# Queueing ScalarE's evacuating copies behind the newest high part, with a look-ahead of six chunks in some stages and four in the others, in an fp32 encoder trunk

## The chip, the cores and the metric

The kernel runs on one core of a Trainium2 chip. The metric is the device time of one execution in microseconds (us). TensorE (PE) multiplies, VectorE (DVE) and ScalarE (ACT) work on what goes into and comes out of the products, GpSimd (POOL) does a few additions, and SyncE (SP) issues most of the DMAs.

## What is computed

The reference is a trunk of two residual layers over 256 tokens of width 2048. Layer 0 mixes tokens by neighbourhood attention, layer 1 by a gated short convolution; each is followed by a gated MLP of inner width 5632. Everything is float32.

```python
def conv_glu_ffn(x, w_up, conv_w, conv_b, w_down):
    h = dwconv_centered(x @ w_up, conv_w) + conv_b
    g, u = jnp.split(h, 2, axis=-1)
    return (jax.nn.silu(g) * u) @ w_down
...
def reference(x, ...):
    h = x
    for i in range(DEPTH):
        a = rms_norm(h, mix_norm[i])
        ...                               # neighborhood_attention, or short_conv_mixer
        h = h + mixed
        h = h + conv_glu_ffn(rms_norm(h, ffn_norm[i]), ffn_w_up[i], ffn_conv_w[i], ffn_conv_b[i], ffn_w_down[i])
    return rms_norm(h, final_norm)
```

## The kernel before

**Numbers in two parts.** Each float32 operand is split into a high part, which ScalarE makes by a cast to a shorter format (the weights' at L185, the activations' at L301), and a low part, the rest, which VectorE makes by a subtraction (L188, L302). A product is the sum of three: high by high, high by low, low by high.

**Chunks.** All weights pass through the core as one list of chunks of 512 KB, in the order in which they are used. For each chunk `prep_to` (L130) writes down a load by SP into one of six `raw` buffers (L164), the cast by ScalarE into one of six `hi` buffers (L185), and the subtraction by VectorE into one of six `lo` buffers (L188). The loads stand in a fixed order on SP's queue. 64 entries of the list are no chunks but jobs ("make", L193): they load three quarter tiles, form three sums on VectorE (L207 to L209) and store them (L214); later stages read the sums back as "kept" chunks.

**Two kinds of stage.** In a `Phase` (L228) the weights are the stationary operand and the 256 tokens stream past them; this is the form of the query and key products (`wqk`), of the short convolution's input (`wsc`) and of the four halves of the up-projections (`wup`: two layers by two halves). An item of a `Phase` is mostly a pair of output tiles: four chunks, 32 matmuls of 512 columns with the high parts (L262), then 32 of 256 columns with the low parts (L270). Each output tile owns one of four `mm` accumulators. In `Values` (L665) and `Tokens` (L387) the activations are stationary and the weights stream: the value products, the attention output, the convolution's output and the four halves of the down-projections (L460 to L462, L686 to L688). Some `Tokens` items (`seven`) take three chunks, one of them kept, and do seven products in place of eight.

**Evacuation.** When an output tile of a `Phase` is done, `both` (L319) evacuates it: ScalarE copies the second half of the accumulator out (L322, tile `corr`), and VectorE adds the first half to it (L323). In the up-projections a chain follows (`up_evac`): scaling (L328), convolution (L336 on ScalarE, L338 twice on VectorE), the gate (L742, L745), the split of the result (L301, L302), and for every second pair of tiles the sums that a `seven` needs (`make_forms`, L517, on POOL) with their splits.

**What sets the order.** The body of L916 to L934 walks the items: it prepares what the item itself needs, writes down its products and evacuations, and then prepares on until `AHEAD` chunks beyond the item's end (jobs do not count). From all that is written down, a scheduler at compile time makes the order of each engine's instructions; the written order is a priority in it, not the order itself. `issue_after(x)` forces an instruction to stand behind `x` on their common engine; it adds no wait on another engine. `newest["ACT"]` is the cast that was written down last. In stages with `self.fence` (every `Phase` but `wqk`) the list `fenced` is filled while an evacuation is written down (L273 to L276), and the splits at L301 and L302 already stand behind the newest cast and the newest subtraction:

```python
            if fenced:
                for x in ("ACT", "DVE"):
                    order.enter_context(tc.issue_after(newest[x].ins))
```

An evacuation is written down before its item's own preparation ahead. With a look-ahead of six, the newest cast is then the one of the second chunk of the following item.

Of the kernel before, what the change touches and what calls it, by code (L numbers as in the profile page):

```python
# [24 lines left out]
S = 256  # L25
# [7 lines left out]
QSCALE = float(128 ** -0.5)  # L33

CH = 8
AHEAD = 6

INTRO = 4
STEP = 4
# [40 lines left out]
def trunk(ctx, tc, xT, par, bias, wqk, wv, wo, wsc, wscout, wup, wdown, out):  # L80
    nc = tc.nc
# [42 lines left out]
    ends = []  # L124
# [5 lines left out]
    def prep_to(n):  # L130
        while len(prepped) < min(n, len(chunks)):
            src, w, kind = chunks[len(prepped)]
            for due in [x for x in stores if x[0] <= len(prepped)]:
                stores.remove(due)
                due[1]()
            if kind == "make":
                make(*src)
                prepped.append(())
                continue
            raw = wp.tile([P, CH * P], F32, name="raw", tag="raw", bufs=RAWS)  # L140
            if kind == "rows":
                load(raw[:, :w], src)
                prepped.append(parts(raw[:, :w]) + (raw,))
                continue

            if kind == "kept":
                t42, left, sums = prepped[-1][2], prepped[-2][2], src()
                load(t42[:, 4 * P:], sums[:, 8 * P:])
                load(raw, sums[:, :8 * P])
                nc.vector.tensor_add(out=t42[:, :4 * P].rearrange("p (f c) -> p f c", f=4),  # L150
                                     in0=t42[:, 4 * P:].rearrange("p (f c) -> p f c", f=4),
                                     in1=left.rearrange("p (f k c) -> p k f c", f=4, c=P)[:, 1])
                prepped.append((parts(raw), parts(t42)))
                continue

            load(raw[:, :4 * w].rearrange("p (f c) -> p f c", f=4), src.rearrange("f p c -> p f c"))
            prepped.append(parts(raw[:, :4 * w].rearrange("p (f k c) -> p f k c", f=4, c=P)) + (raw,))
# [10 lines left out]
    def parts(r):  # L168

        both, low = high_part(r)  # L170
        low()
        return both
# [18 lines left out]
    kept, newest, fenced = {}, {}, []  # L191
# [92 lines left out]
    item = [0]  # L284
    at = [0]

    def tick():
        due = [x for x in later if x[0] <= at[0]]
        later[:] = [x for x in later if x[0] > at[0]]
        for _, fn in due:  # L290
            fn()
        at[0] += 1
# [26 lines left out]
    def both(ps, tag="corr"):  # L319

        corr = tp.tile([P, S], F32, name="corr", tag=tag)
        nc.scalar.copy(out=corr, in_=ps[:, S:])  # L322
        nc.vector.tensor_add(out=corr, in0=ps[:, :S], in1=corr)  # L323
        return corr

    def normed(dst, ps):

        nc.vector.tensor_mul(out=dst, in0=both(ps), in1=rstd)  # L328
# [252 lines left out]
    def qk_evac(f, ps):  # L581
        c = both(ps, "g" if waiting and len(held) % 2 else "corr")
        if waiting:
            held.append(lambda: qk_rest(f, c))
        else:
            qk_rest(f, c)
# [329 lines left out]
    for item[0], (ph, ft, c, k0, ka, kb) in enumerate(items):  # L916

        with ExitStack() as order:
            for x in factor_at:
                order.enter_context(tc.issue_after(x.ins))  # L920
            prep_to(ends[item[0]])
            done = ph.run(ft, c, k0, ka, kb)
            if item[0] != KT // STEP * INTRO:

                if done:
                    order.enter_context(tc.issue_after(done.ins))
                end, n = ends[item[0]], AHEAD
                while n and end < len(chunks):
                    n -= chunks[end][2] != "make"
                    end += 1  # L930
                prep_to(end)
        if item[0] > KT // STEP * INTRO:
            factor_at.clear()
        tick()  # L934
# [70 lines left out]
```

## Time and profile before

| what | value |
|---|---|
| time, median of 3 runs | 2221.36 us (2219.43 to 2226.04) |
| time of the profiled execution | 2221.64 us |
| its span, first to last instruction | 2219.5 us |
| mean granted TensorE clock | 0.996 |
| loads of `raw`, casts L185, subtractions L188 | 920 each |
| copies L322 | 256, of which 224 in fenced stages |

In the profile's timeline a row is: start, duration, engine, line, operation, tiles (out<-in), shape, count, and in brackets the idle time of that engine before it with what ended it. PE is the matmul row of TensorE; its rows overlap a little, since a matmul's end is modelled. SPq and ACTq are DMA issues. A row with a count merges equal neighbours.

The stages of interest lie at these times in the profiled execution: first up-projection half about 397 to 649 us, second 759 to 1010, `wsc` 1126 to 1395, third up-projection half 1481 to 1733, fourth 1843 to 2093. Between them lie `Tokens` stages; queries, keys, values and attention come before 306 us.

### The profile page before, as it was taken

The page shows a single profiled execution, that of the slowest core. Times are in us where ns is not written, and L with a number is a line of the kernel's source. Part 1 is how long each engine was busy: PE and PEld are TensorE (multiplying, and loading weights), DVE is VectorE, ACT ScalarE, POOL GpSimd, SP SyncE. Part 2 cuts the span into 40 slices and gives each one's busy share as a digit, 9 for nine tenths or more (in the row PEclk, how much of TensorE's full clock was granted, in tenths as well). Part 3 has the DMA queues.
Part 4 walks back from the last instruction along what each step waited for, and adds up shares of the span by engine and source line. Part 5 has one row for each costly group of instructions (what it writes and reads, how often), then busy time and mean ns, then how long its engine had stood idle before and what let it go on. Part 6 is the DMA issues. An engine that isn't in the chain of part 4 may idle for free.

```text
span 2219.5 us, 33399 instructions
## 1 busy us (share of the span) xinstructions
PE 2186.1 (98%) x11716; PEld 1891.2 (85%) x11716; DVE 1852.2 (83%) x2842; ACT 1306.1 (59%) x1985; POOL 128.6 (6%) x155
## 2 busy tenths in 40 slices
PE   9999999999999999999999999999999999999998
PEld 8888888888888888888888888888888888888886
DVE  8787667799888978888888777888888898888787
ACT  7555556566665645566655455565666665566565
POOL 0000000001100001210000010000100000010000
PEclk9999999999999999999999999999999999999999
DMA  8777557589758879967778887766986787897575
GB/s 292 231 253 235 188 175 226 195 303 310 250 197 262 284 235 315 316 225 245 247 254 282 292 285 239 236 231 211 301 278 196 231 282 236 293 314 248 182 263 171
DMA packets 362072, 555.34 MB, mean 250 GB/s; under 512 B 21680, under 2 KB 249136, under 8 KB 361904
## 3 DMA queue, kind: packets, MB, share of 16 engines
q1 hardware_dynamic: 332880, 502.23, 69.3%
q10 hardware_dynamic: 29024, 50.98, 6.0%
q8 instruction: 92, 1.51, 0.3%
q14 instruction: 76, 0.62, 0.1%
HBM read 500.70 MB, written 52.43 MB: 249 GB/s over the span
## 4 chain that ended last, share of the span: by engine, by line
PE 84%; DVE 6%; DMA 3%; ACT 3%; issue 2%; POOL 1%; SPq 0%; ACTq 0%; DVEq 0%
PE mm L262 35%; PE mm L270 18%; PE mm L460 6%; PE mm L461 6%; PE mm L462 6%; PE mu L460 3%; DVE lo L188 3%; PE mu L461 3%; PE mu L462 3%; DMA raw<-in_wup 2%; ACT hi L185 2%; PE mm L688 1%; PE mm L686 1%; PE mm L687 1%; DVE conv L338 1%
## 5 line engine op out<-in xcount | busy, mean ns | idle before, releaser
L188 DVE TENSOR_TENSOR lo<-raw,hi 128x1024 fp32r<-128x1024 f32 (+1 forms) x856 | 1019.3, 1211 | 167.5 <-ACT hi L185 74.4
L185 ACT CAST hi<-raw 128x1024 fp32r<-128x1024 f32 (+1 forms) x920 | 918.6, 1012 | 377.8 <-PE mm L462 137.3
L262 PE MATMUL mm<-a,hi 128*128 128x512 f32 x4096 | 970.9, 392 | 17.3 <-ACT hi L185 14.4
L262 PEld LDWEIGHTS mm<-a,hi 128*128 128x128 f32 x4096 | 761.3, 189 | 172.6 <-ACT hi L185 18.1
L270 PEld LDWEIGHTS mm<-a,lo 128*128 128x128 f32 x4096 | 514.5, 191 | 14.0 <-DVE lo L188 1.4
L270 PE MATMUL mm<-a,lo 128*128 128x256 f32 x4096 | 520.1, 283 | 1.1 <-DVE lo L188 1.1
L460 PE MATMUL mm<-hi,act 128*128 128x512 f32 x634 | 247.7, 391 | 2.0 <-ACT hi L185 1.2
L462 PE MATMUL mm<-hi,act 128*128 128x512 f32 x634 | 246.7, 389 | 0.0
L461 PE MATMUL mm<-lo,act 128*128 128x512 f32 x576 | 224.5, 390 | 0.0
L338 DVE SCALAR_TENSOR_TENSOR conv<-pad,pt,conv 128x256 f32<-128x256 f32 x384 | 182.1, 479 | 26.4 <-ACT conv L336 21.2
L322 ACT COPY corr<-mm 128x256 f32<-128x256 f32 x256 | 92.4, 370 | 189.6 <-PE mm L270 185.7
L336 ACT ACTIVATE conv<-pad,pt 128x256 f32<-128x256 f32 x176 | 105.7, 601 | 147.6 <-DVE pad L328 144.8
L460 PEld LDWEIGHTS mm<-hi,act 128*128 128x128 f32 x634 | 119.0, 188 | 28.3 <-DVE corr L323 1.6
L462 PEld LDWEIGHTS mm<-hi,act 128*128 128x128 f32 x634 | 119.0, 188 | 24.7
L461 PEld LDWEIGHTS mm<-lo,act 128*128 128x128 f32 x576 | 108.2, 188 | 21.7
L323 DVE TENSOR_TENSOR corr<-mm,corr 128x256 f32<-128x256 f32 x256 | 106.6, 417 | 19.6 <-ACT corr L322 18.9
L526 POOL TENSOR_TENSOR s<-conv 128x128 f32<-128x128 f32 x27 | 38.4, 1423 | 1018.9 <-DVE conv L745 1018.9
L302 DVE TENSOR_TENSOR act<-conv,act 128x256 fp32r<-128x256 f32 x88 | 39.3, 446 | 50.1 <-ACT act L301 49.9
L328 DVE TENSOR_TENSOR pad<-corr,rstd 128x256 f32<-128x256 f32 x176 | 73.8, 420 | 1.1
L461 PE MATMUL mu<-lo,sf 128*128 128x512 f32 x180 | 70.0, 389 | 0.0
L462 PE MATMUL mu<-hi,sf 128*128 128x512 f32 x180 | 70.0, 389 | 0.0
L460 PE MATMUL mu<-hi,sf 128*128 128x512 f32 x180 | 70.0, 389 | 0.0
(160 smaller groups left out, 1587.1 us busy)
## 6 DMA issues: line engine op xcount, KB each, us to landing
raw<-in_wup SPq DMA_DIRECT2D x352, 512.0 KB, 5.4
raw<-in_wdown SPq DMA_DIRECT2D x124, 512.0 KB, 4.9
kept<-act ACTq DMA_DIRECT2D x192, 256.0 KB, 4.8
raw<-in_wsc SPq DMA_DIRECT2D x96, 512.0 KB, 5.4
act<-in_wdown SPq DMA_DIRECT2D x156, 256.0 KB, 5.9
raw<-kept SPq DMA_DIRECT2D x64, 512.0 KB, 5.0
raw<-in_wqk SPq DMA_DIRECT2D x56, 512.0 KB, 4.8
raw<-in_wv SPq DMA_DIRECT2D x32, 512.0 KB, 4.2
```

Of the source, the lines that this page charges most:

```text
L185: newest["ACT"] = nc.scalar.copy(out=hv, in_=r)
L188: newest["DVE"] = nc.vector.tensor_sub(out=lv, in0=r, in1=hv.bitcast(F32))
L262: nc.tensor.matmul(self.ps[ft], lhsT=prepped[i][0][:, o:o + P], rhs=self.src[k], start=k == 0, stop=False)
L270: nc.tensor.matmul(self.ps[ft][:, S:], lhsT=prepped[i][1][:, o:o + P], rhs=self.src[k][:, :S], start=False, stop=k == self.nk - 1)
L322: nc.scalar.copy(out=corr, in_=ps[:, S:])
L323: nc.vector.tensor_add(out=corr, in0=ps[:, :S], in1=corr)
L328: nc.vector.tensor_mul(out=dst, in0=both(ps), in1=rstd)
L336: nc.scalar.activation(c, x[:, 1:S + 1], AF.Identity, scale=w[1], bias=b)
L338: nc.vector.scalar_tensor_tensor(out=c, in0=x[:, tap:tap + S], scalar=w[tap], in1=c, op0=ALU.mult, op1=ALU.add)
L460: nc.tensor.matmul(ps, lhsT=xh, rhs=wh, start=start, stop=False)
L461: nc.tensor.matmul(ps, lhsT=xh, rhs=wl, start=False, stop=False)
L462: nc.tensor.matmul(ps, lhsT=xl, rhs=wh, start=False, stop=stop)
```

## The change

The copy at L322 is put behind the newest cast where the stage is fenced, as the splits already are. The constant `AHEAD` becomes 4, and a second one, `FURTHER`, is 6 and holds for items whose stage has the fence: `wsc` and the four up-projection halves. `wqk`, `Values` and `Tokens` go from six to four. The number of instructions and their work stay the same.

```diff
-AHEAD = 6
+AHEAD, FURTHER = 4, 6
...
     def both(ps, tag="corr"):
 
         corr = tp.tile([P, S], F32, name="corr", tag=tag)
-        nc.scalar.copy(out=corr, in_=ps[:, S:])
+        with ExitStack() as order:
+            if fenced:
+                order.enter_context(tc.issue_after(newest["ACT"].ins))
+            nc.scalar.copy(out=corr, in_=ps[:, S:])
         nc.vector.tensor_add(out=corr, in0=ps[:, :S], in1=corr)
         return corr
...
-                end, n = ends[item[0]], AHEAD
+                end, n = ends[item[0]], FURTHER if getattr(ph, "fence", False) else AHEAD
                 while n and end < len(chunks):
                     n -= chunks[end][2] != "make"
                     end += 1
```

## The prediction

> **What bounds the kernel now.** I read the page first, then the waits of PE, then the busy time by stage, then the timelines of PE, ACT and SP around the longest waits.
>
> ```profile
> PE 2186.1 (98%) x11716; PEld 1891.2 (85%) x11716; DVE 1852.2 (83%) x2842; ACT 1306.1 (59%) x1985; POOL 128.6 (6%) x155
> ...
> raw<-in_wup SPq DMA_DIRECT2D x352, 512.0 KB, 5.4
> ```
>
> ```profile
> ACT corr L322 <- PE mm L270: 185.7, 147, 5.1
> ACT conv L336 <- DVE pad L328: 144.8, 132, 3.2
> ACT hi L185 <- PE mm L462: 137.3, 126, 2.1
> ```
>
> TensorE is busy for 2186.1 of 2219.5 us, so nothing but its 33.4 us of idle time, and matmuls that run slower than they can, is to be had. ScalarE's longest waits (total, times, longest) are those at the copies of L322, 185.7 us in all, where it stands at a copy whose accumulator isn't finished. That idleness costs only where something behind the copy is wanted. PE's own waits tell where:
>
> ```profile
> PE mm L262 <- ACT hi L185: 14.4, 6, 3.4
> PE mm L262 <- DVE h L357: 2.4, 2, 1.6
> PE tr L639 <- DVE act L302: 1.8, 1, 1.8
> PE o L651 <- DVE act L302: 1.2, 2, 1.1
> PE mm L460 <- ACT hi L185: 1.2, 1, 1.2
> ```
>
> The largest, 14.4 us, is a stationary-weight matmul waiting for a cast. The timeline of PE shows four places that hold nearly all of it, one in each up-projection half, and a row of the same 16 matmuls undisturbed:
>
> ```profile
> 458.53 5.44 PE L262 MATMUL mm<-a,hi 128*128 128x512 f32 x16 [3.39 <-ACT hi L185]
> ...
> 809.31 3.82 PE L262 MATMUL mm<-a,hi 128*128 128x512 f32 x16
> 812.96 2.07 PE L270 MATMUL mm<-a,lo 128*128 128x256 f32 x16
> 818.42 3.94 PE L262 MATMUL mm<-a,hi 128*128 128x512 f32 x16 [3.39 <-ACT hi L185]
> ...
> 1542.61 5.53 PE L262 MATMUL mm<-a,hi 128*128 128x512 f32 x16 [3.39 <-ACT hi L185]
> ...
> 1902.57 5.34 PE L262 MATMUL mm<-a,hi 128*128 128x512 f32 x16 [3.38 <-ACT hi L185]
> ```
>
> The four waits are alike to 0.01 us, so an order of instructions makes them, not a transfer. In three of the four the 16 matmuls behind the wait also take 1.5 to 1.7 us more than the 3.82 of an undisturbed group. Why the cast comes late is seen on ScalarE at the second place, and on SP's queue before it:
>
> ```profile
> 802.02 0.37 ACT L322 COPY corr<-mm 128x256 f32<-128x256 f32 x1 [5.10 <-PE mm L270]
> 802.29 1.05 ACT L185 CAST hi<-raw 128x1024 fp32r<-128x1024 f32 x1
> ...
> 809.89 0.36 ACT L322 COPY corr<-mm 128x256 f32<-128x256 f32 x1
> ...
> 813.26 0.30 ACT L301 CAST act<-s 128x128 fp32r<-128x128 f32 x1
> 814.87 0.60 ACT L336 ACTIVATE conv<-pad,pt 128x256 f32<-128x256 f32 x1 [1.31 <-DVE pad L328]
> 815.37 0.35 ACT L322 COPY corr<-mm 128x256 f32<-128x256 f32 x1
> 817.02 0.42 ACT L742 ACTIVATE g<-conv 128x256 f32<-128x256 f32 x1 [1.29 <-DVE conv L338]
> 817.34 1.03 ACT L185 CAST hi<-raw 128x1024 fp32r<-128x1024 f32 x1
> ...
> 822.48 1.99 ACT L185 CAST hi<-raw 128x1024 fp32r<-128x1024 f32 x2
> ```
>
> ```profile
> 791.24 17.01 SPq L164 DMA_DIRECT2D raw<-in_wup  x4
> ```
>
> The cast at 802.29 stands right behind a copy that idled for 5.10 us until PE was done with an output tile, and PE wants that cast's chunk for its very next item. From then on ScalarE is just in time or late; at 817.34 it is late, since two copies and what hangs on them (L336, L742, each waiting for VectorE) stand ahead of the cast that PE waits for. The data aren't late. Loads, casts and subtractions keep one order, so I matched them by number (920 of each): the chunk cast at 817.34 landed at 795.2 us. The rows bear it out as far as rows can: from 791.24 to 808.25 SP issues four loads of `raw`. Six buffers go round, so the last two of the four had to wait for the subtractions behind the cast of 802.29 and its successor; the first two are the chunk cast at 817.34 and the next one, and a load lands 5.4 us after its issue. ScalarE had some 20 us in which it could have cast them.
>
> **The change part by part.**
>
> *The copy behind the newest cast.* For an evacuation the newest cast is that of the second chunk of the next item (front part: six chunks ahead, four of them used by the item). At the quoted place, the copy of 802.02 and its pair's second must now stand behind the cast of 802.29 and the one after it, and the copies of 809.89 and 815.37 behind the cast of 817.34 and the one after it. What is queued behind the copy on ScalarE is the chain of L336, L742, L301; who waits for that is VectorE, and in the end the down-projection, much later. Matched by number, 16 of the 224 copies in fenced stages now stand ahead of their newest cast: one in `wsc`, 15 in the four up-projection halves, all within some 30 us of the first job of the stage. For the other 208 the edge asks for what is already so. (In the first item of the two halves without an introduction, the stage before now prepares only that item's own four chunks, and the edge asks for nothing.) For each of the 16 the chunk concerned had landed 9.8 us or more before the copy ran, so the copy waits for no DMA, only for one or two casts of 1.05 us.
>
> What this brings: PE's four waits, 3.39 + 3.39 + 3.39 + 3.38 = 13.55 us, and the slow matmuls behind them, (5.44 + 3.94 + 5.53 + 5.34) - 4 x 3.82 = 4.97 us; together 18.5 us. What is late next: after 813.56, where the splits of the forms end (813.26 + 0.30), ScalarE can cast at once, from 813.6 to 814.6, while PE's own low-part matmuls run to 812.96 + 2.07 = 815.0. So the wait goes to nothing, with 0.4 us in hand even where the splits stay ahead of the cast. What the copies lose: 809.89 becomes about 815.7 (two casts from 813.6), 5.8 us later. Its cover is the accumulator's own slack:
>
> ```profile
> 538.16 7.28 PE mm L262 x32
> 545.44 3.83 PE mm L270 x32
> ```
>
> In the chain of waits (start, duration) an undisturbed pair of tiles takes 7.28 + 3.83 = 11.1 us and there are four accumulators, so a tile of one pair is written again only when the next pair is through. The next pair would begin at 815.0, the one after it at 826.1; the delayed copies and their additions are over by about 817. I cost the delay at nothing. On VectorE the additions L323 wait with the copies, and subtractions stand behind them; PE wants the first of these when it turns to the low parts, 3.65 us into the item (818.7) if it keeps to single tiles as at 809.31, else 7.28, and the casts are over at 815.7: 3 us for a subtraction that follows its cast at once, so nothing again.
>
> [...]
>
> *Four in place of six in the other stages.* Nothing in the trace shows a look-ahead of four, so I bound it. Busy time by stage (duration, then PE's busy time) shows what there is to win or disturb:
>
> ```profile
> 649.00:759.00 110.00, 110.00 (x488) 91.14 (x487) 96.42 (x108) 69.42 (x77) 0.00 (x0) 1.00 0.82 267
> ```
>
> A `Tokens` stage like 649 to 759 has PE busy for 110.00 of 110.00 us: nothing to gain there. All waits of PE that lie in or at the end of stages without the fence are 2.4 + 1.8 + 1.2 + 1.2 = 6.6 us, from the list of waits; that is the end on the side of gain. On the other side: how far ahead a cast really runs.
>
> ```profile
> 707.15 1.05 ACT L185 CAST hi<-raw 128x1024 fp32r<-128x1024 f32 x1 [2.10 <-PE mm L462]
> 709.92 1.05 ACT L185 CAST hi<-raw 128x1024 fp32r<-128x1024 f32 x1 [1.71 <-PE mm L462]
> ...
> 715.12 0.39 PE L460 MATMUL mu<-hi,act 128*128 128x512 f32 x1
> ```
>
> These casts begin when PE ends a chunk, 2.77 us apart: the free buffer binds them, not the written order. The list of ScalarE's waits agrees: 137.3 us before casts ended with PE's L462. A cast such as that of 709.92 ends at 710.97 and is wanted at 715.12, 4.1 us later (by number; the least in three of the four down-projections). If two chunks less of look-ahead took two chunks, 2 x 2.77 = 5.5 us, off that, PE would wait 1.4 us at such a place. Between a gain of 6.6 us and a loss I take zero, by the row nearest to it: a limit that the buffers set before the six does isn't moved by a four. Loads are not touched, since SP's order is fixed and six `raw` buffers allow what they allowed.
>
> *The sum.* 2221.64 us of the profiled execution (which stands 0.3 us over the median of the runs, and 2.1 over its own span) less 18.5 is 2203.1; I forecast 2203.
>
> **The rivals.**
>
> *The wait moves on to the next cast* (slightly faster, hardly measurable). The cast of 822.48 is the third of the item and stands behind the split L301 of the tile before, 822.48 - 815.37 = 7.1 us behind that tile's copy. If the scheduler keeps that sequence, the second copy goes to about 816.0, this cast ends at 816.0 + 7.1 + 1.05 = 824.2, and PE, which begins the item at 815.0, wants it after 16 + 16 matmuls (3.65 from 809.31 to 812.96, and half of 3.83), at 820.6: 3.6 us are paid again, at four places 14.4, and the time is 2203.1 + 14.4 = 2217.5. For it: the scheduler left casts behind such chains before. Against: the copies and their chains now come later in its plan too, while the cast keeps its own ready time.
>
> *Accumulators* (no change to be measured). If the delayed copies held PE for their 5.8 us at each of four places, 23 us would be paid and the time be 2203.1 + 23.2 = 2226. The 11.1 us pair speaks against; it decides only where the casts come 9 us later than I have them. [...]
>
> *Four chunks are too few* (slower). In the streaming stages each `seven` wants four casts nearly at once. If every one of the 64 found its cast 1.4 us late, that is 90 us and 2203 + 90 = 2293; from (18.5 + 6.7) / 1.4 = 18 such places on the change is measurably slower. For it: the least lead of 4.1 us is under two chunks. Against: the casts wait for buffers, and PE idles for 0.00 us in those stages.
>
> *Values gain as well* (faster still). If fewer early subtractions let the splits L302 for L639 and L651 pass, and the stage ends too, up to 6.6 us more go: 2196.5.
>
> *The edge does nothing* (2221.6). If the late casts had another cause than the copy ahead of them, the four waits stay.
>
> **How the numbers follow.** 0.3% of the time, 6.7 us, is about what a measurement can tell from no change, so faster means under 2214.7. Forecast 0.62; further gain of `Values` 0.13; wait moved on 0.10; accumulators 0.03; edge without effect 0.04; four too few 0.08. Faster is 0.62 + 0.13 and a small part of the moved wait, 0.76; same 0.16; slower 0.08. The range goes from 2196.5, the whole gain of the other stages, to 2217.5, the moved wait; it leaves out the accumulators, the edge without effect and the slower case, and a little below.
>
> **What would show it.** Right: in the timeline no row of L262 with 3.39 us behind a cast; PE's waits for L185 at L262 fall from 14.4 to under 2 us; at the first job of each up-projection half two casts stand ahead of each pair's copies; PE's busy time equals the stage's length in the four halves; ScalarE's idle time before L322 falls little. Wrong: a new wait of PE on L185 some 6 us after the old places (the wait moved), waits of L262 that end with L322 or L323 (accumulators), or new waits at L460 and L686 in the streaming stages (four too few).

## The result and the profile after

The changed kernel takes 2199.83 us (median of 4 runs, 2198.87 to 2200.89) against 2222.4 us of the kernel before beside it; the ratio is 0.9898, with a 95% interval of 0.9881 to 0.9915. The profiled execution has 2200.17 us and a span of 2198.3 us, 21.2 us less than the span before; the mean granted clock went from 0.996 to 0.998. The forecast was 2203.0.

Lines after 322 of the changed file are numbered 3 higher: the copy is L325, the addition behind it L326, the residuals' addition L360.

The busy times on the page, then PE's waits (total, times, longest; the lines left out are 3.5 us at the start and in the tail), in the kernel after:

```profile
PE 2181.9 (99%) x11716; PEld 1890.5 (86%) x11716; DVE 1845.1 (84%) x2842; ACT 1298.4 (59%) x1985; POOL 128.5 (6%) x155
```

```profile
PE mm L270 <- DVE lo L188: 5.0, 3, 3.4
...
PE mm L262 <- DVE a L310: 0.8, 2, 0.5
PE mm L463 <- DVE corr L326: 0.3, 1, 0.3
```

The wait of L262 for the cast, 14.4 us before, is gone altogether. So are those for the residuals (2.4 us), the splits (1.8 and 1.2) and the cast at the streaming matmul (1.2). One line is new in size: the low-part matmuls L270 wait 5.0 us for subtractions (1.1 before). The other two lines are small.

ScalarE and PE at the second of the four places, the one the prediction worked through, in the timeline of the kernel after:

```profile
803.23 0.30 ACT L301 CAST act<-s 128x128 fp32r<-128x128 f32 x1
803.43 1.99 ACT L185 CAST hi<-raw 128x1024 fp32r<-128x1024 f32 x2
805.33 0.36 ACT L325 COPY corr<-mm 128x256 f32<-128x256 f32 x1
806.08 0.37 ACT L325 COPY corr<-mm 128x256 f32<-128x256 f32 x1 [0.39 <-PE mm L270]
```

```profile
798.40 2.08 PE L270 MATMUL mm<-a,lo 128*128 128x256 f32 x16
...
805.88 3.82 PE L262 MATMUL mm<-a,hi 128*128 128x512 f32 x16
```

Two casts now stand ahead of the pair's copies, right behind the split of the forms. They end at 805.42 (the first at about 804.5), and PE begins the item that wants the first at 805.88 with no idle time. The first copy's tile was through at 798.40 + 2.08 = 800.48 and is copied at 805.33, 4.9 us later.

The stages show what is left. Busy time of the first and second up-projection half after (duration, then PE's busy time; the granted clock follows the five engines):

```profile
393.00:640.00 247.00, 247.00 (x1427) 218.56 (x1426) 215.12 (x370) 150.01 (x247) 23.74 (x28) 1.00 0.78 258
750.00:1002.00 252.00, 247.29 (x1410) 218.12 (x1409) 216.50 (x362) 143.95 (x232) 24.12 (x28) 0.99 0.82 270
```

The first half has no idle time. The second has lost its old wait and has 4.71 us of new ones.

To put a price on each place I added up, over all matmuls in both traces, how much later each starts than an undisturbed one of its size (227 ns after 512 columns, 120 after 256). Before, this comes to about 42 us, after to about 21; how a change from one size to the other is counted moves these totals by some 2 us and the pieces by some tenths. The four old places give 19.0 us back, their slow matmuls included. The stages without the fence and their ends give about 8.6: 3.4 where the attention waited for splits, in the first 172 us; 2.7 where the stages at 1126 and 1481 waited for residuals; 2.5 at 1013 and 1067 us, inside the streaming stage behind the second half. In the second half two small old waits give 2.0 and new ones take 7 (waits of 1.26 us at 862 and 3.45 at 888, and slow matmuls behind); several small ones elsewhere take 1.5. The sum, -19.0 - 8.6 - 2.0 + 7 + 1.5 = -21.1, is the 21.2 us of the span but for 0.1.

### The profile page after: what moved, and what is told of

The parts are those of the page before. It is cut to its first block, busy times and chain, and to the rows that moved or that the text cites. A ratio compares the mean times of both kernels' runs of the same rounds, so it can differ in the third digit from the quotient of the medians.

```text
span 2198.3 us, 33402 instructions
## 1 busy us (share of the span) xinstructions
PE 2181.9 (99%) x11716; PEld 1890.5 (86%) x11716; DVE 1845.1 (84%) x2842; ACT 1298.4 (59%) x1985; POOL 128.5 (6%) x155
## 4 chain that ended last, share of the span: by engine, by line
PE 88%; DMA 5%; DVE 3%; issue 1%; ACT 1%; SPq 0%; POOL 0%; ACTq 0%; DVEq 0%
PE mm L262 36%; PE mm L270 19%; PE mm L463 7%; PE mm L464 6%; PE mm L465 6%; DMA raw<-in_wup 3%; PE mu L463 3%; PE mu L465 3%; PE mu L464 3%; PE mm L689 1%; PE mm L691 1%; PE mm L690 1%; DMA kept<-act 1%; DMA act<-in_wdown 1%; DVE lo L188 1%
## 5 line engine op out<-in xcount | busy, mean ns | idle before, releaser
L262 PE MATMUL mm<-a,hi 128*128 128x512 f32 x4096 | 964.8, 391 | 0.8 <-DVE a L310 0.8
L262 PEld LDWEIGHTS mm<-a,hi 128*128 128x128 f32 x4096 | 760.0, 188 | 153.2 <-DVE a L310 1.9
L270 PEld LDWEIGHTS mm<-a,lo 128*128 128x128 f32 x4096 | 514.5, 191 | 19.0 <-DVE lo L188 6.1
L270 PE MATMUL mm<-a,lo 128*128 128x256 f32 x4096 | 521.4, 283 | 5.1 <-DVE lo L188 5.0
L463 PE MATMUL mm<-hi,act 128*128 128x512 f32 x634 | 247.7, 391 | 0.6 <-DVE corr L326 0.3
L339 ACT ACTIVATE conv<-pad,pt 128x256 f32<-128x256 f32 x176 | 103.8, 600 | 187.7 <-DVE pad L331 187.6
L325 ACT COPY corr<-mm 128x256 f32<-128x256 f32 x256 | 90.4, 369 | 135.7 <-PE mm L270 131.9
L463 PEld LDWEIGHTS mm<-hi,act 128*128 128x128 f32 x634 | 119.1, 188 | 26.5 <-DVE corr L326 2.2
L326 DVE TENSOR_TENSOR corr<-mm,corr 128x256 f32<-128x256 f32 x256 | 106.4, 420 | 28.2 <-ACT corr L325 27.6
L463 PE MATMUL mu<-hi,sf 128*128 128x512 f32 x180 | 70.0, 389 | 0.0
```

The costliest lines, as they stand in the source:

```text
L262: nc.tensor.matmul(self.ps[ft], lhsT=prepped[i][0][:, o:o + P], rhs=self.src[k], start=k == 0, stop=False)
L270: nc.tensor.matmul(self.ps[ft][:, S:], lhsT=prepped[i][1][:, o:o + P], rhs=self.src[k][:, :S], start=False, stop=k == self.nk - 1)
L339: nc.scalar.activation(c, x[:, 1:S + 1], AF.Identity, scale=w[1], bias=b)
L463: nc.tensor.matmul(ps, lhsT=xh, rhs=wh, start=start, stop=False)
```

## The experiments

Runs of the kernel before, beside the experiments, had medians of 2220.4 to 2221.3 us; ratios are against these. A difference is a difference of medians.

**The fence alone.** Six chunks everywhere, the copy behind the newest cast:

```diff
-AHEAD, FURTHER = 4, 6
+AHEAD, FURTHER = 6, 6
```

> The copies of L322 stand behind the newest cast; the look-ahead stays six everywhere. Theory (a copy that idles for its accumulator blocks the cast that PE wants): the four waits of 3.39 us are gone, PE's waits outside the fenced stages (splits L302 before L639 and L651, residual L357 before L262, together 5 to 6 us) stay as before; time of before less 18 us, about 2204. Rival (the look-ahead of four does the work, by taking early casts and subtractions out of the way): no change, about 2222, the four waits stay.

2209.74 us (2208.76 to 2210.93), ratio 0.9947 [0.9933, 0.9961]. From its list of PE's waits:

```profile
PE mm L270 <- DVE lo L188: 4.4, 4, 3.4
PE mm L262 <- DVE h L360: 3.8, 2, 2.0
```

No wait of L262 for the cast is left, so the fence by itself removes all four. But it brings the new subtraction wait with it, and the waits outside the fenced stages stay, those for residuals (the second line) and those for splits.

**The look-ahead alone.** Four and six, the copy free:

```diff
-            if fenced:
-                order.enter_context(tc.issue_after(newest["ACT"].ins))
             nc.scalar.copy(out=corr, in_=ps[:, S:])
```

> The look-ahead is four outside the fenced stages and six in them; the copies aren't fenced. Theory: the four waits of 3.39 us and the slow matmuls behind them stay (18.5 us), only waits outside the fenced stages change, 3 to 7 us of gain, 2215 to 2219. Rival (look-ahead does the work): about 2200.

2213.89 us (2211.59 to 2216.51), ratio 0.9967 [0.9956, 0.9979]. From its waits of PE:

```profile
PE mm L262 <- ACT hi L185: 13.5, 4, 3.4
```

The reverse picture: the four waits stay, the outside ones go but for 0.7 us. The look-ahead alone is worth 7.4 us, which I had costed at nothing. The two parts alone save 11.6 and 7.4 us, 19.0 together, the whole change 22.6 (2222.4 - 2199.83): neither takes anything from the other.

**Four chunks everywhere, with and without the fence.** If the look-ahead in the fenced stages also shrinks to an item's own four chunks:

```diff
-AHEAD, FURTHER = 4, 6
+AHEAD, FURTHER = 4, 4
```

> Both: the fence, but a look-ahead of four in the fenced stages too. The newest cast is then the last one of the item's own four chunks, so the edge asks for nothing that the item's products don't ask for. Theory: casts of the next item fall behind copies again, waits of L262 for L185 of 13 us or more, 2214 to 2225. Rival (any look-ahead does, the fence alone frees ScalarE): 2198 to 2204.

2261.36 us (2260.71 to 2262.35), ratio 1.0180 [1.0166, 1.0194]: the slowest of all, and far above both expectations. From its waits of PE, and ScalarE at the first place in its timeline:

```profile
PE mm L262 <- ACT hi L185: 50.8, 10, 7.0
```

```profile
447.51 0.30 ACT L301 CAST act<-s 128x128 fp32r<-128x128 f32 x1
447.72 1.99 ACT L185 CAST hi<-raw 128x1024 fp32r<-128x1024 f32 x2
```

When the evacuation is written down, the newest cast is the item's own last one, and the fence asks for what is so anyway. The next item's casts stand behind the whole chain of both tiles, whose last split ends at 447.81, and PE waits 7 us for the first of them, then 5.3 for the same thing one item on, at each of the four halves. The same kernel without the fence:

> A look-ahead of four everywhere and no fence at L322. Theory (with four chunks ahead the newest cast is one of the item's own, and the fence at L322 asks for nothing): the same as the four-everywhere kernel with the fence, 2258 to 2265, with the same waits of L262 for L185, about 51 us. Rival (the fence itself did the harm there): clearly faster than that, 2214 to 2235.

2260.78 us (2259.57 to 2261.48), ratio 1.0178 [1.0161, 1.0195]: no difference. With four chunks the fence does nothing; it works because the two chunks beyond the item give it something to stand behind.

**Eight in the fenced stages.** If accumulators held by late copies cost anything, two more casts ahead of the copies must show it:

```diff
-AHEAD, FURTHER = 4, 6
+AHEAD, FURTHER = 4, 8
```

> The changed kernel with a look-ahead of eight in the fenced stages: each copy must stand behind the cast of the last chunk of the next item, two casts later than with six. Theory (accumulators have 11 us of slack; a later copy costs nothing by itself): no wait of L262 that ends with L322 or its addition; only in the dense second half, where casts wait for loads, some us more, 2198 to 2208. Rival (accumulators are held too long): waits of L262 for the copy or its addition in all four halves, 2215 or more.

2196.76 us (2192.45 to 2198.80), ratio 0.9888 [0.9874, 0.9903], not to be told from six. In the profiled execution, the fastest of the four, PE waits neither for a copy or its addition at L262 nor for a subtraction at L270. The 2215 of the rival did not come. But the run tests that rival less than was meant, because on the whole its copies are not later. Matched by number with their tiles, the latest copy of the second half comes 8.5 us after its tile is through, with six chunks 13.3. Only in the first items of `wsc` and of the first and third halves are the latest copies later with eight, by some 2.6 us (12.3 us against 9.6 in `wsc`). What speaks against the accumulators is above all the kernel after itself.

**Five and three outside the fenced stages.**

```diff
-AHEAD, FURTHER = 4, 6
+AHEAD, FURTHER = 5, 6        (and, in another kernel, 3, 6)
```

> The kernel after with a look-ahead of five in place of four outside the fenced stages. With six there the time was 2209.7, with four 2199.8. Theory one, that each chunk less of look-ahead lets more splits and residuals pass ahead of the casts, by degrees: 2203 to 2207. Theory two, that only the order at a few stage edges matters, which flips at one value: 2198 to 2201 or 2208 to 2211, with either none or nearly all of the waits at L642, L654 and of L262 for the residual.

> The kernel after with a look-ahead of three in place of four outside the fenced stages. Theory one, that less is better there as long as the buffers and not the number bind the casts: 2197 to 2201, no new wait at L463. Theory two, that three is less than one item's chunks, so that a cast is written down behind the evacuation that it should precede: waits of L463 and L688 for L185 of 1 to 2 us at many places, 2206 to 2240.

Five: 2204.43 us (2202.70 to 2206.51), ratio 0.9927 [0.9913, 0.9941]. Three: 2201.33 us (2200.62 to 2205.44), ratio 0.9918 [0.9904, 0.9932]. With the 2209.74 of six and the 2199.83 of four: it falls by degrees down to four, and three can't be told from four. In the list of waits of five chunks, those of L262 for residuals are down from 3.8 us to nothing, those of L642 for splits from 1.9 to 0.8, while those of L654 are still 2.2; in the list of three chunks none of these lines is there. Three doesn't starve the streaming matmuls: no wait of L463 for a cast.

**The sums of the second half spread out.** The new waits lie where the second half has its jobs packed into its first items. Spread over more of them:

```diff
-                  jobs=take(UP_JOBS[2 * layer + half]), hosts=(3, 16) if half else (8, 22))
+                  jobs=take(UP_JOBS[2 * layer + half]), hosts=(3, 20) if half else (8, 22))
```

> The changed kernel with the jobs of the second half of each layer spread over items 3 to 20 in place of 3 to 16. The changed kernel lost some 7 us in the second up-projection half to subtractions that came late (waits of L270 for L188, 5.0 us, and slow matmuls behind). Theory (the jobs' loads and sums, 13 in 13 items, hold up the weights' loads and VectorE): these waits fall under 2 us and the time to 2192 to 2197. Rival (an accident of the order, not of the load): waits stay at 4 us or more, or go elsewhere, 2199 to 2203.

2190.61 us (2190.05 to 2191.33), ratio 0.9861 [0.9848, 0.9875]: faster than both kernels, and its interval lies wholly under that of the change. Its stage of the second half:

```profile
740.00:992.00 252.00, 252.00 (x1431) 222.22 (x1430) 223.04 (x368) 148.82 (x235) 22.06 (x28) 1.00 0.84 277
```

PE is busy for 252.00 of 252.00 us, and what is left of its waits, 4.1 us, belongs to the start and the tail.

**The sums left out.** Is it the sums on VectorE, or the transfers that come with them? In the kernel after, the 13 jobs of the second half form no sums and store the three quarter tiles as they were loaded; loads and stores stay:

```diff
         def adds():
+            if 18 <= no < 31:
+                return
```

> The changed kernel without the sums L207 to L209 of the 13 jobs of the second up-projection half (their loads and stores stay; what is stored there is the raw quarter tiles). VectorE has 27 us less to do there, the DMAs the same. Theory A (weights' loads are late, casts wait for them at the head of ScalarE's queue, and the splits and subtractions behind fall late): the waits of L270 for L188 stay, 3 us or more, 2196 to 2201. Theory B (VectorE is full): they are gone, 2192 to 2195.

2192.33 us (2190.64 to 2192.38), ratio 0.9869 [0.9854, 0.9884]. Of the 5.0 us of L270's waits 0.3 are left. My first theory, of loads that come late whatever becomes of the sums, falls: with the same transfers and no sums the wait is gone. That does not show that VectorE was full: without sums the stores, and the loads behind them, need not wait for VectorE either. What the timelines say stands further below.

**The sums doubled, in the spread kernel.** The reverse: three more VectorE operations of the same size for each of those jobs:

```diff
                 nc.vector.tensor_add(out=t, in0=l, in1=t)
+                if 18 <= no < 31:
+                    for x in (l, r, t):
+                        nc.vector.tensor_max(out=x, in0=x, in1=x)
```

> The kernel with the jobs spread over items 3 to 20, and in the second up-projection half each job's three sums followed by three elementwise operations of the same size that change nothing: VectorE has 27 us more to do there, the DMAs the same. Theory A (late loads): no wait of L270 for L188 comes back, 2189 to 2193. Theory B (VectorE is full): waits of L270 for L188 come back, 2195 or more.

2207.61 us (2207.18 to 2208.16), ratio 0.9940 [0.9925, 0.9955], 17 us over the spread kernel, and the wait is back (lines shifted by 4):

```profile
PE mm L274 <- DVE lo L188: 8.7, 7, 1.7
```

**The spread kernel without the fence, and with eight.**

> The kernel after with the sums of the second up-projection half spread over more items, and the copies of the stationary-weight stages again free of the newest cast; look-ahead four and six as after. Theory one, that the late cast at each first job is made by the copies ahead of it and the sums only crowded VectorE: all four waits of L262 for L185 of about 3.4 us come back, some 18 us over the spread kernel with the edge (2190.6), so 2205 to 2211. Theory two, that the sums' work near the job is what made the cast late, so that the edge is needless once they are spread: the two places of the second halves lose their wait and the time is 2190 to 2200.

> The spread kernel with a look-ahead of eight in place of six in the fenced stages. Theory one, that both cure the same thing (VectorE late with subtractions in the second up-projection half): no wait is left there to take away, so the time is that of the spread kernel, 2188 to 2192. Theory two, that they cure different things and add up: the 3 us that eight brought over six come on top, 2185.5 to 2188.

Without the fence: 2214.11 us (2213.13 to 2216.00), ratio 0.9975 [0.9960, 0.9989], 23.5 us over the spread kernel, with the four waits back (the others are 0.7 us at L639 and the 3.5 at the start and in the tail):

```profile
PE mm L262 <- ACT hi L185: 13.5, 4, 3.4
```

So the late cast at the first job does not come from the sums being packed: spreading them without the fence gains nothing over the look-ahead alone (2213.89). The 23.5 are more than the 18 expected, because more of the matmuls behind the waits ran slow (below). With eight: 2191.51 us (2191.27 to 2192.57), ratio 0.9869 [0.9855, 0.9882]. Spreading and eight don't add up; the first is enough.

## Why the prediction was right, and where it was not

**Its main term was right, in size and mechanism.** 13.55 us of waits and 4.97 of slow matmuls, 18.5, were to go; 19.0 went. At the second place PE was to have 0.4 us in hand when the first of the two casts ended; it has 805.88 - 804.5 = 1.4. The fence does it, not the look-ahead and not the spacing of the jobs: the four waits of 3.4 us are gone in every kernel with the fence and six or eight chunks, and there, or longer, in every one without it.

**The copies' delay costs nothing, as said.** The copy that was to come 5.8 us later comes 4.4 us later against the end of its tile (4.9 us behind it, 0.4 before), and no list shows L262 waiting for L325 or L326. With four accumulators, putting the copies some 5 us later at four places was worth about 19 us here.

The slack has an end, though. At 886.13 in the kernel after (rows below) the first of two copies comes 13.3 us after its tile was through, more than the 11.1 of a pair; no wait for an accumulator can show there, since PE already waits for a subtraction. And there is one kind of place where an accumulator is waited for, before as after: where a streaming stage begins, its matmuls wait for the additions that free the last tiles' accumulators. That is the 0.3 us of L463 in the list after, 0.6 before (`PE mm L460 <- DVE corr L323`), 1.1 with the fence alone and 1.0 with eight chunks.

**The step on VectorE failed.** "3 us for a subtraction that follows its cast at once, so nothing again" held at the places that I had looked at, the first jobs. At 888 us, some items later in the second half, it doesn't. From the timeline of the kernel after, SP, ScalarE, VectorE and PE:

```profile
870.95 4.17 SPq L164 DMA_DIRECT2D act<-in_wdown  x3
875.21 2.56 SPq L164 DMA_DIRECT2D raw<-in_wup  x3
```

```profile
876.68 1.05 ACT L185 CAST hi<-raw 128x1024 fp32r<-128x1024 f32 x1
...
882.91 1.05 ACT L185 CAST hi<-raw 128x1024 fp32r<-128x1024 f32 x1 [5.17 <-DMA raw<-in_wup]
883.86 0.40 ACT L301 CAST act<-conv 128x256 fp32r<-128x256 f32 x1
...
885.52 0.51 ACT L301 CAST sf<-s 128x384 fp32r<-128x384 f32 x1
...
886.13 0.64 ACT L325 COPY corr<-mm 128x256 f32<-128x256 f32 x2
```

```profile
884.29 0.42 DVE L302 TENSOR_TENSOR act<-conv,act 128x256 fp32r<-128x256 f32 x1 [2.92 <-ACT act L301]
886.06 0.56 DVE L302 TENSOR_TENSOR sf<-s,sf 128x384 fp32r<-128x384 f32 x1 [1.34 <-ACT sf L301]
...
886.74 0.42 DVE L326 TENSOR_TENSOR corr<-mm,corr 128x256 f32<-128x256 f32 x1
887.07 1.22 DVE L188 TENSOR_TENSOR lo<-raw,hi 128x1024 fp32r<-128x1024 f32 x1
```

```profile
888.34 1.32 PE L270 MATMUL mm<-a,lo 128*128 128x256 f32 x8 [3.45 <-DVE lo L188]
```

The subtraction that PE wants is that of the chunk cast at 876.68 (matched by number); its cast was done at 877.7. It runs at 887.07, since it stands on VectorE behind splits and an addition. The splits wait for ScalarE's part of them, 2.92 and 1.34 us; that part stands behind two casts, and the first of these waits 5.17 us for its load.

Nearly the same order stood there before (the second split came ahead of the second cast). ScalarE and VectorE at the same chunks in the kernel before:

```profile
890.43 1.06 ACT L185 CAST hi<-raw 128x1024 fp32r<-128x1024 f32 x1 [3.42 <-DMA raw<-in_wup]
...
892.31 1.05 ACT L185 CAST hi<-raw 128x1024 fp32r<-128x1024 f32 x1
893.26 0.63 ACT L322 COPY corr<-mm 128x256 f32<-128x256 f32 x2
```

```profile
891.82 0.42 DVE L302 TENSOR_TENSOR act<-conv,act 128x256 fp32r<-128x256 f32 x1 [2.98 <-ACT act L301]
...
893.97 0.42 DVE L323 TENSOR_TENSOR corr<-mm,corr 128x256 f32<-128x256 f32 x1
894.31 1.21 DVE L188 TENSOR_TENSOR lo<-raw,hi 128x1024 fp32r<-128x1024 f32 x1
```

Here too the copies stand behind these two casts, without any edge. Matched by number, the edge asks the copies of 886.13 only to stand behind a cast that was over at 871.36, before their tiles were through. So it is the compile-time order, not the edge, that holds these copies, and "the copy waits for no DMA", said of the 16 copies that the edge moves, is not what failed. What differs is when the load of the first cast came. In us from PE's end of the previous pair of tiles, matched by number in each trace:

| kernel | load issued | its cast begins | subtraction that PE wants, done | PE wants it |
|---|---|---|---|---|
| before | -3.5 | 4.4 | 9.5 | 10.0 |
| look-ahead alone | -4.1 | 3.5 | 8.6 | 10.0 |
| fence alone | 0.4 | 8.2 | 13.5 | 10.0 |
| after | 0.5 | 8.2 | 13.5 | 10.0 |
| after, eight chunks | -4.5 | 2.5 | 5.0 | 10.0 |
| after, sums spread out | -6.2 | 0.3 | 7.3 | 10.0 |
| after, sums left out | -10.1 | -2.6 | 2.2 | 10.0 |

Before, the subtraction had 0.5 us in hand. After, the load comes 4.0 us later, and PE waits 3.45. The load was issued at 875.21, behind the three loads of a job, and SP's waits in that stretch say what for:

```profile
SPq L164 <- DMA kept<-act: 5.5, 2, 2.8
```

The quarter tiles of a job come free when the sums of an earlier one are stored. How often SP waits for such stores does not tell by itself: in the whole second half 51.0 us in 25 times after and 31.1 in 10 with the sums spread out, but also 46.7 in 17 before and 51.1 in 19 with the look-ahead alone, where the subtraction comes in time.

With the sums as they are, this load is late with the fence at six chunks and in time without it; it is early and the wait gone when the sums are left out (7.5 us less) or spread out (9.2 less); doubled sums cost 17 more. How the fence makes the load late was not tried apart. As the timelines read, the slip goes round: a late subtraction frees the buffer of a later load late (SP waits 1.7 us for one between 866 and 876), and that load stands behind a job's loads on SP's queue. VectorE was not full at 884: it idled 2.92 + 1.34 us at operations that were not ready. The term was mis-sized: 0 in the sum, +7 in the second half.

**The term for the look-ahead was mis-sized too.** Zero was taken "by the row nearest to it: a limit that the buffers set before the six does isn't moved by a four". That holds in the middle of a streaming stage, where the row came from, and not at its ends (one of the gains, at 1067 us, lies inside such a stage). VectorE and PE at the end of the stage that `wsc` follows, before:

```profile
1118.11 3.49 DVE L188 TENSOR_TENSOR lo<-raw,hi 128x1024 fp32r<-128x1024 f32 x3
1122.21 1.23 DVE L188 TENSOR_TENSOR lo<-raw,hi 128x1024 fp32r<-128x1024 f32 x1 [0.61 <-ACT hi L185]
...
1125.15 0.68 DVE L357 TENSOR_TENSOR h<-mm,h 128x512 f32<-128x512 f32 x1
```

```profile
1125.98 2.08 PE L262 MATMUL mm<-a,hi 128*128 128x512 f32 x8 [0.77 <-DVE h L357]
```

VectorE in the same place after:

```profile
1108.43 2.36 DVE L188 TENSOR_TENSOR lo<-raw,hi 128x1024 fp32r<-128x1024 f32 x2
...
1112.50 0.68 DVE L360 TENSOR_TENSOR h<-mm,h 128x512 f32<-128x512 f32 x1
```

Four subtractions, one of them waiting for its cast, stood ahead of the residual's additions; now there are two, 2 x 1.2 + 0.6 = 3 us less, and PE goes on without a gap at 1115.37. Six, five, four chunks give 2209.7, 2204.4, 2199.8. The bound of 6.6 us, from PE's listed waits, was short too: by starts of matmuls the gain is 8.6, since each of these waits costs some 0.16 us beyond its listed idle time, and the 0.6 us of L460 for the copies' additions should have been in the list.

**The sum.** The two errors, 8.6 us of gain and 7 - 2.0 + 1.5 = 6.5 us of cost left out, nearly cancel: the total was 3 us off, its parts by up to 8.6. The main term was foreseen; that the number came out this near is luck. The rival `Values` was right about what happened, and the new waits hid it in the total.

**The other rivals.** The wait didn't move on to the next cast. Four chunks were not too few in the streaming stages, nor are three; they are in the fenced ones, at 2261, in the place I had not priced because the change leaves six there. Of the signs named, PE's busy time fills the first and the third half, lacks 0.4 us in the fourth and 4.7 in the second. ScalarE's idle time before the copies was to fall little; it fell from 185.7 to 131.9. From the waits of ACT after:

```profile
ACT conv L339 <- DVE pad L331: 187.6, 132, 3.3
ACT corr L325 <- PE mm L270: 131.9, 113, 4.4
```

The idle time moved: the convolution behind the copy has 187.6 (144.8 before).

**Open.** Why the compile-time order puts the cast behind the copies only at the first job of a half, how the fence makes the load at 888 us late, and why eight chunks bring it early again, was not settled.

## What to carry to other kernels

Look for the instruction that the bottleneck wants next, and for what stands ahead of it on its engine that isn't ready, like the copies and their chain ahead of the cast of 817.34, whose chunk had landed at 795.2; here, moving evacuations that had slack behind them was worth the whole wait and the slow matmuls after it. Such an edge needs work beyond the item to stand behind (six chunks, not four). Then look along the whole stage, not only at the old wait: a subtraction that had 0.5 us in hand before was 3.5 us late after, since its neighbour's load had slipped by 4. Give each stage its own look-ahead: preparation that runs too far ahead stands before the small operations at a stage's end.

## What the runs showed of the hardware

In these traces a wait of PE costs more than its idle time, by an amount that varies. The next matmul starts 0.15 to 0.16 us later than the listed idle time accounts for, at each wait over 0.2 us before and after; what comes on top is in the matmuls behind. After the same 3.39 us, the 16 matmuls took 3.94 us at one place before and 6.49 in the kernel with the look-ahead alone. The stretches behind these two waits, before and then in that kernel (duration, PE's busy time, four more engines, the granted clock):

```profile
818.00:826.00 8.00, 7.58 (x40) 6.53 (x41) 6.92 (x10) 5.17 (x7) 0.00 (x0) 1.00 0.73 250
```

```profile
815.00:823.00 8.00, 7.78 (x29) 6.46 (x30) 6.93 (x10) 4.96 (x7) 0.00 (x0) 0.64 0.81 262
```

At a clock of 1.00 the starts behind the wait are 225 to 236 ns apart, but for the first, at 335; at 0.64, 11 in a row come 427 ns apart in place of 227, about half the speed. The kernel before shows both: in the 6 us from 458, 1542 and 1902 the granted clock is 0.72 each time and the 16 matmuls take 5.44, 5.53 and 5.34 us, in the 6 us from 818 it is 1.00 and they take 3.94. Over the four waits this came to 5 us before and 8.7 in the spread kernel without the fence, with the same idle time (13.5 us in both). What decides after which wait the clock is lower, no run here shows.
